# A two-layer hybrid decoder trunk on one core: order of the up-projection's matmuls, time of the parameter loads, queue of the output stores

## The chip, the core and the metric

One core of a Trainium2 chip runs the whole program. The metric is the time of one execution on the device in microseconds (us), as the median of several runs. A profile of one execution stands beside it; its span (from the first to the last instruction) is a little shorter than the execution's time.

## What is computed

The input x has 256 rows (positions) of 1024 numbers. Cut to what matters:

```
layer 0:  h = rmsnorm(x) ; u = h @ ab_w_in        # 1024 -> 2560 columns
          ya = conformer_conv(u_val, u_gate)      # GLU, causal conv of width 31, layernorm, silu
          yb = attention(q, k, v)                 # 8 heads of 64, causal, ALiBi
          x = x + concat(ya, yb) @ ab_w_out
          x = x + square(relu(rmsnorm(x) @ w_up[0])) @ w_down[0]      # 1024 -> 4096 -> 1024
layer 1:  h = rmsnorm(x) ; gate, xr = split(h @ c_w_in)
          xr = conv of width 4 ; y = rg_lru(xr) * gelu(gate)
          x = x + y @ c_w_out
          x = x + square(relu(rmsnorm(x) @ w_up[1])) @ w_down[1]
out = rmsnorm(x)
```

All in float32. With 256 rows there is one attention block, so no past blocks are selected.

## The kernel before, in words

**Planner.** The body of `hybrid_trunk` doesn't issue instructions. Each helper (`mms`, `tt`, `act`, `move`, `dma`, ...) adds an operation to a `Plan` with its engine, operands and an estimated cost. `Plan.schedule` (line 132) simulates the engines, lets each one pick the ready operation of highest rank, and `emit` issues everything in the order found. SP's DMAs alone keep the order in which they were added. So a moved line in the body moves work on every engine only as far as the planner's ranks let it. Nearly all instructions are issued at line 312, so rows of the profile are told apart by their tiles.

**Layout.** Activations lie transposed, as eight chunks (`xT[k]`, 128 channels x 256 positions). Weights come by SP's queue in pieces of 1 MB into the five `raw` tiles (or into pairs of `wh` and `wl`). Where a piece is split, ScalarE or VectorE rounds it into `wh` (fp32r) and VectorE puts the rest into `wl` (lines 588 to 592). The activations are split in the same way into a high and a low half, which lie side by side in one tile (`split_act`, line 701). A product is then three terms: high x wh, low x wh, high x wl.

**MLP (lines 982 to 1011).** For each of 32 groups f of 128 hidden channels, `project_wide` (line 695) makes the up-projection: for each of the eight chunks one matmul of 512 columns (`wh` against high and low side by side) and one of 256 columns (`wl` against high), both into one PSUM bank (bank_b). VectorE and ScalarE then make the activation. Four groups later the down-projection of the group (`down_mm`, line 1019) follows: twelve matmuls of 512 columns, three for each of four blocks, into four standing accumulators (bank_a). The last four groups' down-projection (`TAIL`) is done block by block behind the loop: 48 matmuls. In rows of the profile, `bank_b<-x,wh` with 512 columns and `bank_b<-x,wl` with 256 are the up-projection, `bank_a<-wh,f` and `bank_a<-wl,f` the down-projection; the layer-1 projections have `bank_b<-x,wh` with 256 columns.

**Start (lines 653 to 678, 738 to 750, 795 to 802).** SP loads x in four parts (arena), each followed by a part of the first gate and value weights. GpSimd's queue issues nine small loads, which wait for nothing but two memsets: the convolution's weights into `wrow`, eight vectors of parameters into rows of `prow`. TensorE transposes x chunk by chunk (`x_chunk`, line 739; bank_a<-ident,arena) and multiplies each chunk into the first gate and value units (bank_b<-xg,raw). Then it transposes `wrow` and `prow` into one bank, from which VectorE copies them into columns (`wcol`, `pcol`).

**End (lines 1212 to 1229).** The last down-projection goes block by block; each half row block of the output is scaled and stored by two DMAs on SP's queue:

```
        act(xg[:, :512], xg[:, :512], AF.Copy, scale=fc[:, 6:7])
        stt(xg[:, 512:], b, fc[:, 6:7], gfin[:, 512:], OP.mult, OP.mult)
        for h in (slice(0, 512), slice(512, D)):
            dma(o_dst[:, t, h], xg[:, h], P * 2048)
```

Of the kernel before, what the change touches and what calls it, by code (L numbers as in the profile page):

```python
# [11 lines left out]
P = 128  # L12
S = 256
D = 1024
KD = D // P
NF = 4096 // P
CONVW = 31
# [4 lines left out]
ARENA = 10496  # L22


WARM, XP, SIDE = 10, 4, (0, 0, 0, 0)


SETS = {AF.Exp: "exp", AF.Tanh: "exp", AF.Sqrt: "sqrt", AF.Silu: "silu",
# [288 lines left out]
def fsize(ap):  # L317
    n = 1
    for d in ap.shape[1:]:
        n *= d  # L320
    return n


def is_psum(ap):
    return str(ap.space).endswith("PSUM")
# [3 lines left out]
def hybrid_trunk(ctx, tc, x, mix_norm, mlp_norm, w_up, w_down, ab_w_in, ab_conv_w, ab_ln_g, ab_ln_b,  # L329
# [3 lines left out]
    plan = Plan(nc)  # L333
# [4 lines left out]
    def tl(name, shape=(P, S), dt=F32):  # L338
        return sb.tile(list(shape), dt, name=name)
# [23 lines left out]
    def vcost(n, fast=False, ap=False):  # L363
        return 0.066 + n * (0.00052 if fast else 0.001042) + ((0.105 if fast else 0.062) if ap else 0.0)

    def tt(out, a, b, op, engs="V"):
        n = fsize(out)
        cost = {}
        if "V" in engs:
            cost["V"] = vcost(n)  # L370
        if "G" in engs:
            cost["G"] = 0.135 + n * 0.0021
        return plan.add(engs, [("tensor_tensor", (out, a, b), {"op": op})], [out], [a, b], cost)

    def stt(out, a, s, b, op0, op1):
        ins = [a, b] + ([s] if isap(s) else [])
        return plan.add("V", [("scalar_tensor_tensor", (out, a, s, b), {"op0": op0, "op1": op1})], [out], ins,
                        {"V": vcost(fsize(out), ap=isap(s))})
# [9 lines left out]
    def copy(out, a):  # L388
        return plan.add("V", [("tensor_copy", (out, a), {})], [out], [a], {"V": vcost(fsize(out), not is_psum(a))})

    def move(out, a, scale=None):

        n, ap, far = fsize(out), scale is not None, not is_psum(a)

        def go(e, sub):
            if e is nc.scalar:
                return e.activation(sub(out), sub(a), AF.Copy, **({"scale": scale} if ap else {}))  # L397
            return e.tensor_scalar(sub(out), sub(a), scale, None, op0=OP.mult) if ap else e.tensor_copy(sub(out), sub(a))  # L398

        return plan.add("VA", [(go, (), {})], [out], [a] + ([scale] if ap else []),  # L400
                        {"V": vcost(n, far, ap), "A": (0.092 if far else 0.05) + n * 0.000833 + 0.093 * ap}, AF.Copy)
# [12 lines left out]
    def memset(out, v, engs="G"):  # L414
        return plan.add(engs, [("memset", (out, v), {})], [out], [], {engs: 0.1 + fsize(out) * 0.0005})

    def mms(items, after=()):

        calls, outs, ins, c = [], [], [], 0.0
        for o, l, r, st, sp in items:  # L420
            calls.append(("matmul", (o,), {"lhsT": l, "rhs": r, "start": st, "stop": sp, "skip_group_check": True}))
            outs.append(o)
            ins += [l, r]
            c += max(fsize(r) / 2400.0, 0.0533) * (1 if l.dtype == F32R else 4) + (0.0135 if l.dtype == F32R else 0.005)
        return plan.add("T", calls, outs[:1], ins, {"T": c}, after=after)

    def transposes(items):
        calls = [("transpose", (o, i, d), {}) for o, i, d in items]
        return plan.add("T", calls, [items[0][0]], [i for _, i, _ in items] + [items[0][2]],
                        {"T": 0.109 * len(items)})  # L430
# [3 lines left out]
        return plan.add("T", [("matmul", (out,), {"lhsT": in_, "rhs": ident, "start": first, "stop": False, "is_transpose": True,  # L434
                                                  "skip_group_check": True})], [out], [in_, ident], {"T": 0.109})

    def small_dma(out, in_):

        return plan.add("G", [("dma_start", (out, in_), {})], [out], [in_], {"G": 0.55}, lag=4.0)

    def dma(out, in_, size):
        return plan.add("S", [("dma_start", (out, in_), {})], [out], [in_], {"S": 0.0}, size=size)


    ident = tl("ident", (P, P))
    ones = tl("ones", (P, P))
    pcol = tl("pcol", (P, P))
# [26 lines left out]
    def ar(*shape):  # L474
        n = 1
        for d in shape:
            n *= d
        assert top[0] + n <= ARENA, top[0] + n
        a = arena[:, top[0]:top[0] + n]
        top[0] += n  # L480
        if len(shape) == 2:
            a = a.rearrange("p (a b) -> p a b", a=shape[0])
        return a
# [20 lines left out]
    def bank(tag):  # L504
        t = banks[tag][bank_at[tag] % len(banks[tag])]
        bank_at[tag] += 1
        return t
# [135 lines left out]
    xrow = [ar(2, D // XP) for _ in range(XP)]  # L643
    xall = arena[:, base0:base0 + 2 * D].rearrange("p (h t d) -> p h t d", h=XP, t=2)
    mrow, prow, wrow, scr, diag = ar(P), ar(P), ar(P), ar(XP, D // XP), ar(2, P)
    xsrc = x[0].rearrange("(t p) d -> p t d", p=P)
    R = lambda ap: ap.rearrange("a (b p) -> (a b) p", p=P)
# [13 lines left out]
    b = bank("b")  # L661
# [5 lines left out]
        mms([(warm[:, :P], ones, ones, True, True)])  # L667
    memset(prow, 0.0)
    memset(wrow, 0.0)
    small_dma(wrow[:CONVW * 4], R(ab_conv_w[0]))  # L670
    col0 = {"mix": 0}
    r0 = 16
    for name, ap, n in (("mlp", R(mlp_norm), 16), ("lng", R(ab_ln_g), 4), ("lnb", R(ab_ln_b), 4),
                        ("cw", R(c_conv_w[0]), 32), ("cb", R(c_conv_b), 8), ("br", c_b_r[0], 8),
                        ("bi", c_b_i[0], 8), ("lam", R(c_lambda), 8)):
        small_dma(prow[r0:r0 + n], ap)
        col0[name] = r0
        r0 += n

    def par(name, c):  # L680
        i = col0[name] + c
        return pcol[:, i:i + 1]
# [12 lines left out]
    def project_wide(b, u, xs):  # L695

        w = weights(u)
        for k in range(KD):
            mms([(b, w[0][:, k, :], xs[k][2], k == 0, False), (b[:, :S], w[1][:, k, :], xs[k][0], False, k == KD - 1)])

    def split_act(src, scale, tag, bufs, engs="V"):
        t = rot(tag, bufs, (P, 2 * S), F32R)
# [9 lines left out]
    def scaled(src, scale):  # L712
        t = rot("xg", KD)
        move(t, src, scale)
        return t
# [22 lines left out]
    xs = {}  # L738
    def x_chunk(k):
        b = bank("a")  # L740
        transposes([(b[:, t * P:(t + 1) * P], xrow[k * XP // KD][:, t, k % (KD // XP) * P:(k % (KD // XP) + 1) * P], ident) for t in range(2)])
        xs[k] = scaled(b[:, :S], par("mix", k))
        move(xT[k], b[:, :S])

    for k in range(KD):
        x_chunk(k)
    vgb = {0: (bank("b"), bank("b"))}
    for k in range(KD):
        for b, u in zip(vgb[0], (u_gate[0], u_val[0])):
# [16 lines left out]
    def gate_tail(c):  # L766
        gt = gts[c % 2]
        tt(gt, vgb[c][0][:, :S], rstd, OP.mult)
        act(gt, gt, AF.Tanh, scale=0.5)
# [4 lines left out]
    def val_tail(c):  # L774

        stt(gts[c % 2], gts[c % 2], 1.0, rstd, OP.add, OP.mult)
        tt(z[:, c, CONVW - 1:], vgb[c][1][:, :S], gts[c % 2], OP.mult)

        aside = SIDE[c]
        for j in range(CONVW):  # L780
            src = z[:, c, j:j + S]
            w = wcol[:, j * 4 + c:j * 4 + c + 1]
            if j < aside:
                t = yside[c % 2] if j == 0 else prod[j % 3]
                act(t, src, AF.Copy, scale=w)
                if j:
                    tt(yside[c % 2], yside[c % 2], t, OP.add, "G")
            elif j == aside:
                ts(y[c], src, w, None, OP.mult)
            else:  # L790
                stt(y[c], src, w, y[c], OP.mult, OP.add)
        if aside:
            tt(y[c], y[c], yside[c % 2], OP.add)

    b = bank("a")
    for t in range(2):
        mms([(b[:, t * P:(t + 1) * P], ones, diag[:, t], t == 0, True)])
    transposes([(b[:, 256:384], wrow, ident)])
    transposes([(b[:, 384:512], prow, ident)])
    copy(rstd, b[:, :S])  # L800
    ts(wcol, b[:, 256:384], 0.5, None, OP.mult)
    copy(pcol[:, 16:], b[:, 400:512])
    gate_tail(0)
    val_tail(0)

# [91 lines left out]
    for i in range(4):  # L899
        weights(u_v[i])  # L900
        n, j = units[u_v[i]]
        w = homes[n][j].rearrange("p (a b) -> p a b", a=2)
        for a in range(2):
            k = 2 * i + a
# [73 lines left out]
    xs = {}  # L978
# [58 lines left out]
    xs = {}  # L1037
# [11 lines left out]
    for n, block in enumerate(blocks):  # L1049
        t, c0, c1, b = block  # L1050
# [137 lines left out]
    xs = {}  # L1188
# [22 lines left out]
    o_dst = out[0].rearrange("(t p) d -> p t d", p=P)  # L1211
    for n, block in enumerate(blocks):
        t, c0, c1, b = block
        xg, fc = xg2[t], fcol[:, t]
        for i in range(len(us)):
            down_mm(block, ws[i], hs[i], False, i == len(us) - 1)

        part = fc[:, n % 2:n % 2 + 1]
        act(fsq, b, AF.Square, accum=part)
        if c0 == 0:  # L1220
            tt(xg[:, :512], b, gfin[:, :512], OP.mult)
            ts(fc[:, 4:5], part, 1.0 / D, EPS, OP.mult, OP.add)
            continue
        act(fc[:, 5:6], part, AF.Sqrt, scale=1.0 / D, bias=fc[:, 4:5])
        recip(fc[:, 6:7], fc[:, 5:6])
        act(xg[:, :512], xg[:, :512], AF.Copy, scale=fc[:, 6:7])
        stt(xg[:, 512:], b, fc[:, 6:7], gfin[:, 512:], OP.mult, OP.mult)
        for h in (slice(0, 512), slice(512, D)):
            dma(o_dst[:, t, h], xg[:, h], P * 2048)
    hybrid_trunk.plan = plan.emit(renew)  # L1230


# [29 lines left out]
```

## Time and profile before

| | |
|---|---|
| median of 3 runs | 573.44 us (573.37 to 573.73) |
| the profiled execution | 573.54 us |
| its span | 571.8 us |
| TensorE busy (matmuls; weight loads) | 563.5 us (99%); 480.8 us (84%) |
| VectorE, ScalarE, GpSimd busy | 434.4, 301.8, 7.5 us |
| DMA | 98.70 MB, mean 173 GB/s |

Busy times of TensorE are of modelled ends, so the pace of matmuls is read from the distance of their starts. A chain of waits is followed back from the last instruction to what released each one.

### The profile page before, as it was taken

To read this page: it belongs to the slowest core of one execution; us is meant where nothing else is said; L and a number is where in the kernel's file an instruction comes from. 1 tells how busy PE (TensorE), PEld (TensorE's weight loads), DVE (VectorE), ACT (ScalarE), POOL (GpSimd) and SP (SyncE) were. 2 spreads that over 40 slices of the span, in tenths; PEclk is the share of its full clock that TensorE was granted. 3 is DMA by queue.
4 is the path that set the end of the run, shared out by engine and by line. 5 is a ranking of instruction groups with operands and counts; after the bars stand their busy time and mean duration, and the time that the engine had idled before them with its cause. 6 is when DMAs were issued, how large, how long until landed. Compare 5 with 4: busy or idle time off the path is not lost.

```text
span 571.8 us, 8523 instructions
## 1 busy us (share of the span) xinstructions
PE 563.5 (99%) x2985; PEld 480.8 (84%) x2985; DVE 434.4 (76%) x987; ACT 301.8 (53%) x618; POOL 7.5 (1%) x31
## 2 busy tenths in 40 slices
PE   8999999999999999999999999999999999999995
PEld 7888759988888888888889999888888888888884
DVE  2899998889767677777739997979776777777732
ACT  5104134657555555555538799637455555555523
POOL 5000000000000000000000000000000000000000
PEclk9999999999999999999999999999999999999999
DMA  8991593415665466555009746955545664662001
GB/s 237 306 379 42 160 317 113 147 40 183 192 219 178 156 202 211 169 184 184 0 2 287 229 144 209 367 201 173 196 149 186 212 192 147 202 229 86 1 0 74
DMA packets 71738, 98.70 MB, mean 173 GB/s; under 512 B 3368, under 2 KB 59776, under 8 KB 71696
## 3 DMA queue, kind: packets, MB, share of 16 engines
q1 hardware_dynamic: 71408, 98.06, 53.2%
q8 instruction: 23, 0.38, 0.3%
q0 software_dynamic: 288, 0.11, 0.1%
q14 instruction: 19, 0.16, 0.1%
HBM read 97.11 MB, written 1.05 MB: 172 GB/s over the span
## 4 chain that ended last, share of the span: by engine, by line
PE 97%; DMA 1%; SPq 1%; DVE 0%; issue 0%; ACT 0%; DVEq 0%; ACTq 0%
PE bank_b L312 53%; PE bank_a L312 44%; DMA arena<-in_x_dram 1%; SPq L312 1%; DVE arena L312 0%; DVE x L398 0%; DVE x L312 0%; ACT tiny L312 0%; ACT arena L312 0%; DVE tiny L312 0%; DVEq L398 0%; ACTq L312 0%
## 5 line engine op out<-in xcount | busy, mean ns | idle before, releaser
L312 DVE TENSOR_TENSOR wl<-raw,wh 128x512 fp32r<-128x512 f32 x296 | 201.3, 689 | 78.3 <-ACT wh L397 65.6
L397 ACT ACTIVATE wh<-raw 128x512 fp32r<-128x512 f32 x259 | 160.9, 630 | 159.4 <-PE bank_b L312 95.2
L312 PE MATMUL bank_b<-x,wh 128*128 128x512 f32 (+1 forms) x768 | 230.5, 361 | 0.0
L312 PE MATMUL bank_b<-x,wl 128*128 128x256 f32 x640 | 179.6, 281 | 0.0
L312 PE MATMUL bank_a<-wh,f 128*128 128x512 f32 x512 | 160.2, 394 | 0.0
L312 PEld LDWEIGHTS bank_b<-x,wh 128*128 128x128 f32 x768 | 136.4, 189 | 23.4 <-DVE arena L312 0.2
L312 PEld LDWEIGHTS bank_b<-x,wl 128*128 128x128 f32 x640 | 121.1, 189 | 2.2
L312 PEld LDWEIGHTS bank_a<-wh,f 128*128 128x128 f32 x512 | 92.2, 188 | 19.4
L312 PE MATMUL bank_a<-wl,f 128*128 128x512 f32 x256 | 100.6, 393 | 0.0
L312 PEld LDWEIGHTS bank_a<-wl,f 128*128 128x128 f32 x256 | 48.0, 188 | 11.9
L312 DVE SCALAR_TENSOR_TENSOR arena<-arena,wcol 128x256 f32<-128x256 f32 x120 | 50.5, 478 | 0.2
L312 PE MATMUL bank_b<-xg,raw 128*128 128x256 f32 x160 | 35.8, 380 | 0.0
L312 PEld LDWEIGHTS bank_b<-xg,raw 128*128 128x128 f32 x160 | 29.9, 190 | 3.9
L312 ACT ACTIVATE relu<-relu 128x256 f32<-128x256 f32 x64 | 26.1, 410 | 12.4 <-DVE relu L312 12.2
L312 DVE TENSOR_TENSOR relu<-bank_b,relu 128x256 f32<-128x256 f32 x64 | 26.8, 418 | 5.0 <-ACT relu L312 5.0
L312 DVE TENSOR_TENSOR f<-relu,f 128x256 fp32r<-128x256 f32 x64 | 26.8, 422 | 2.2 <-ACT f L397 2.2
L312 DVE SCALAR_TENSOR_TENSOR relu<-relu,rstd 128x256 f32<-128x256 f32 x64 | 26.8, 425 | 1.8
L312 ACT ACTIVATE arena<-arena 128x256 f32<-128x256 f32 (+2 forms) x39 | 19.3, 521 | 16.8 <-DVE arena L312 15.6
L312 ACT ACTIVATE relu<-bank_b 128x256 f32<-128x256 f32 x64 | 23.6, 368 | 5.7 <-PE bank_b L312 5.7
L312 PE MATMUL bank_a<-arena,wl 128*128 128x256 f32 x96 | 26.3, 379 | 0.0
L312 PE MATMUL bank_a<-arena,wh 128*128 128x256 f32 x96 | 26.3, 378 | 0.0
L312 ACT ACT_TABLE_LOAD x17 | 21.8, 1283 | 1.9 <-PE bank_b L312 0.9
(127 smaller groups left out, 434.7 us busy)
## 6 DMA issues: line engine op xcount, KB each, us to landing
raw<-in_w_up_dram SPq DMA_DIRECT2D x64, 512.0 KB, 5.5
raw<-in_w_down_dram SPq DMA_DIRECT2D x64, 512.0 KB, 4.3
raw<-in_c_w_in_dram SPq DMA_DIRECT2D x16, 512.0 KB, 7.7
raw<-in_ab_w_in_dram SPq DMA_DIRECT2D x8, 512.0 KB, 7.7
wh<-in_ab_w_in_dram SPq DMA_DIRECT2D x5, 512.0 KB, 8.5
wl<-in_ab_w_in_dram SPq DMA_DIRECT2D x5, 512.0 KB, 8.6
raw<-in_ab_w_out_dram SPq DMA_DIRECT2D x4, 512.0 KB, 10.5
wh<-in_c_w_out_dram SPq DMA_DIRECT2D x4, 512.0 KB, 3.4
```

Of the source, the lines that this page charges most:

```text
L312: r.append(getattr(self.engines[o.eng], method)(*map(sub, a), **{n: sub(v) for n, v in k.items()}))
L397: return e.activation(sub(out), sub(a), AF.Copy, **({"scale": scale} if ap else {}))
```

## The change

In `project_wide` the wide and narrow matmuls of a unit are added in groups: wide ones in pairs, narrow ones in fours, all wide ones first. The nine small loads are added behind the chunks of x and wait for the transposes of chunk 5 (`LATE`); the transpose of `prow` gets a bank of its own and is added later. Of each row block's two stores, the first is issued by ScalarE's queue.

```
--- before.py
+++ after.py
@@ -22,7 +22,7 @@
 ARENA = 10496
 
 
-WARM, XP, SIDE = 10, 4, (0, 0, 0, 0)
+WARM, XP, SIDE, LATE = 10, 4, (0, 0, 0, 0), 5
 
 
 SETS = {AF.Exp: "exp", AF.Tanh: "exp", AF.Sqrt: "sqrt", AF.Silu: "silu",
@@ -434,9 +434,9 @@
         return plan.add("T", [("matmul", (out,), {"lhsT": in_, "rhs": ident, "start": first, "stop": False, "is_transpose": True,
                                                   "skip_group_check": True})], [out], [in_, ident], {"T": 0.109})
 
-    def small_dma(out, in_):
-
-        return plan.add("G", [("dma_start", (out, in_), {})], [out], [in_], {"G": 0.55}, lag=4.0)
+    def small_dma(out, in_, after=()):
+
+        return plan.add("G", [("dma_start", (out, in_), {})], [out], [in_], {"G": 0.55}, after=after, lag=4.0)
 
     def dma(out, in_, size):
         return plan.add("S", [("dma_start", (out, in_), {})], [out], [in_], {"S": 0.0}, size=size)
@@ -667,15 +667,7 @@
         mms([(warm[:, :P], ones, ones, True, True)])
     memset(prow, 0.0)
     memset(wrow, 0.0)
-    small_dma(wrow[:CONVW * 4], R(ab_conv_w[0]))
     col0 = {"mix": 0}
-    r0 = 16
-    for name, ap, n in (("mlp", R(mlp_norm), 16), ("lng", R(ab_ln_g), 4), ("lnb", R(ab_ln_b), 4),
-                        ("cw", R(c_conv_w[0]), 32), ("cb", R(c_conv_b), 8), ("br", c_b_r[0], 8),
-                        ("bi", c_b_i[0], 8), ("lam", R(c_lambda), 8)):
-        small_dma(prow[r0:r0 + n], ap)
-        col0[name] = r0
-        r0 += n
 
     def par(name, c):
         i = col0[name] + c
@@ -695,8 +687,10 @@
     def project_wide(b, u, xs):
 
         w = weights(u)
-        for k in range(KD):
-            mms([(b, w[0][:, k, :], xs[k][2], k == 0, False), (b[:, :S], w[1][:, k, :], xs[k][0], False, k == KD - 1)])
+        for k in range(0, KD, 2):
+            mms([(b, w[0][:, j, :], xs[j][2], j == 0, False) for j in (k, k + 1)])
+        for k in range(0, KD, 4):
+            mms([(b[:, :S], w[1][:, j, :], xs[j][0], False, j == KD - 1) for j in range(k, k + 4)])
 
     def split_act(src, scale, tag, bufs, engs="V"):
         t = rot(tag, bufs, (P, 2 * S), F32R)
@@ -738,12 +732,24 @@
     xs = {}
     def x_chunk(k):
         b = bank("a")
-        transposes([(b[:, t * P:(t + 1) * P], xrow[k * XP // KD][:, t, k % (KD // XP) * P:(k % (KD // XP) + 1) * P], ident) for t in range(2)])
+        turned = transposes([(b[:, t * P:(t + 1) * P], xrow[k * XP // KD][:, t, k % (KD // XP) * P:(k % (KD // XP) + 1) * P], ident) for t in range(2)])
         xs[k] = scaled(b[:, :S], par("mix", k))
         move(xT[k], b[:, :S])
+        return turned
 
     for k in range(KD):
-        x_chunk(k)
+        t = x_chunk(k)
+        if k == LATE:
+            turned = t
+
+    small_dma(wrow[:CONVW * 4], R(ab_conv_w[0]), [turned])
+    r0 = 16
+    for name, ap, n in (("mlp", R(mlp_norm), 16), ("lng", R(ab_ln_g), 4), ("lnb", R(ab_ln_b), 4),
+                        ("cw", R(c_conv_w[0]), 32), ("cb", R(c_conv_b), 8), ("br", c_b_r[0], 8),
+                        ("bi", c_b_i[0], 8), ("lam", R(c_lambda), 8)):
+        small_dma(prow[r0:r0 + n], ap, [turned])
+        col0[name] = r0
+        r0 += n
     vgb = {0: (bank("b"), bank("b"))}
     for k in range(KD):
         for b, u in zip(vgb[0], (u_gate[0], u_val[0])):
@@ -796,12 +802,13 @@
     for t in range(2):
         mms([(b[:, t * P:(t + 1) * P], ones, diag[:, t], t == 0, True)])
     transposes([(b[:, 256:384], wrow, ident)])
-    transposes([(b[:, 384:512], prow, ident)])
     copy(rstd, b[:, :S])
     ts(wcol, b[:, 256:384], 0.5, None, OP.mult)
-    copy(pcol[:, 16:], b[:, 400:512])
     gate_tail(0)
     val_tail(0)
+    b = bank("a")
+    transposes([(b[:, :P], prow, ident)])
+    copy(pcol[:, 16:], b[:, 16:P])
 
 
 
@@ -1225,8 +1232,8 @@
         recip(fc[:, 6:7], fc[:, 5:6])
         act(xg[:, :512], xg[:, :512], AF.Copy, scale=fc[:, 6:7])
         stt(xg[:, 512:], b, fc[:, 6:7], gfin[:, 512:], OP.mult, OP.mult)
-        for h in (slice(0, 512), slice(512, D)):
-            dma(o_dst[:, t, h], xg[:, h], P * 2048)
+        plan.add("A", [("dma_start", (o_dst[:, t, :512], xg[:, :512]), {})], [], [xg[:, :512]], {"A": 0.76})
+        dma(o_dst[:, t, 512:], xg[:, 512:], P * 2048)
     hybrid_trunk.plan = plan.emit(renew)
```

The order in which the engines get their instructions shows it at three places. On TensorE, in the MLP of layer 0, one up unit (bank_b, `x` are the split chunks) stood so before:

```order
L312 MATMUL bank_b_108<-x_130,wh_1_459 128x512
L312 MATMUL bank_b_108<-x_130,wl_1_633 128x256
L312 MATMUL bank_b_108<-x_131,wh_1_459 128x512
L312 MATMUL bank_b_108<-x_131,wl_1_633 128x256
L312 MATMUL bank_b_108<-x_132,wh_1_459 128x512
L312 MATMUL bank_b_108<-x_132,wl_1_633 128x256
L312 MATMUL bank_b_108<-x_133,wh_1_459 128x512
L312 MATMUL bank_b_108<-x_133,wl_1_633 128x256
```

and stands so now, the end of the eight wide ones, the eight narrow ones and the first of the down-projection:

```order
L312 MATMUL bank_b_108<-x_128,wh_1_459 128x512
L312 MATMUL bank_b_108<-x_129,wh_1_459 128x512
L312 MATMUL bank_b_108<-x_130,wl_1_633 128x256
L312 MATMUL bank_b_108<-x_131,wl_1_633 128x256
L312 MATMUL bank_b_108<-x_132,wl_1_633 128x256
L312 MATMUL bank_b_108<-x_133,wl_1_633 128x256
L312 MATMUL bank_b_108<-x_126,wl_1_633 128x256
L312 MATMUL bank_b_108<-x_127,wl_1_633 128x256
L312 MATMUL bank_b_108<-x_128,wl_1_633 128x256
L312 MATMUL bank_b_108<-x_129,wl_1_633 128x256
L312 MATMUL bank_a_104<-wh_1_977,f_137 128x512 x2
```

Every unit of both MLPs is regrouped in this way. On GpSimd's queue (POOL), at the start, the nine small loads pass behind two memsets:

```order
 L312 MEMSET arena 128x128 x2
+L312 MEMSET arena 128x4x30
+L312 MEMSET qs 64x1 x8
 L312 DMA arena<-in_ab_conv_w_dram 124x128
 L312 DMA arena<-in_mlp_norm_dram 16x128
```

They keep their order among themselves. On TensorE, at the start, behind the first gate and value units (bank_a_104 takes the row sums and the transposed `wrow`; bank_b_110 is the second gate unit):

```order
 L312 MATMUL bank_a_104<-arena,ones 128x128 x2
-L312 MATMUL bank_a_104<-ident,arena 128x128 x2
+L312 MATMUL bank_a_104<-ident,arena 128x128
 L312 MATMUL bank_b_110<-xg_118,raw_71 128x256
...
 L312 MATMUL bank_b_110<-xg_123,raw_71 128x256
 L312 MATMUL bank_b_110<-xg_124,raw_71 128x256
+L312 MATMUL bank_a_105<-ident,arena 128x128
 L312 MATMUL bank_b_110<-xg_125,raw_71 128x256
```

The transpose of `prow` leaves its place beside that of `wrow` and stands before the last matmul of the second gate unit.

## Rows read from the trace of the kernel before

**Rows 1.** Of the page, parts 1 and 4: busy times; shares of the chain by engine

```profile
PE 563.5 (99%) x2985; PEld 480.8 (84%) x2985; DVE 434.4 (76%) x987; ACT 301.8 (53%) x618; POOL 7.5 (1%) x31
...
PE 97%; DMA 1%; SPq 1%; DVE 0%; issue 0%; ACT 0%; DVEq 0%; ACTq 0%
```

**Rows 2.** The chain in order of time, MLP of layer 0: start, us, what

```profile
139.97 2.81 PE bank_b L312 x16
142.78 2.78 PE bank_a L312 x12
```

**Rows 3.** Busy time by stretch: us; PE, PEld, DVE, ACT, POOL busy; granted clock; DMA share, GB/s

```profile
123.00:137.00 14.00, 14.00 (x82) 12.29 (x81) 13.83 (x31) 11.12 (x24) 0.00 (x0) 1.00 0.48 154
...
139.81:285.24 145.43, 145.43 (x730) 122.20 (x729) 107.89 (x211) 79.18 (x159) 0.00 (x0) 1.00 0.53 170
403.85:549.28 145.43, 145.43 (x729) 122.19 (x728) 102.54 (x205) 76.83 (x154) 0.00 (x0) 1.00 0.47 153
```

**Rows 4.** Timeline, TensorE, 288 to 300 us: start, us, operation, shape, count

```profile
288.05 0.64 PE L312 MATMUL bank_a<-wh,f 128*128 128x512 f32 x2
288.52 0.40 PE L312 MATMUL bank_a<-wl,f 128*128 128x512 f32 x1
...
290.83 0.62 PE L312 MATMUL bank_a<-wh,f 128*128 128x512 f32 x2
...
298.76 0.39 PE L312 MATMUL bank_a<-wl,f 128*128 128x512 f32 x1
```

**Rows 5.** Timeline, TensorE, layer 1's projections: 256 columns alone

```profile
344.77 0.40 PE L312 MATMUL bank_b<-x,wh 128*128 128x256 f32 x2
...
346.21 0.40 PE L312 MATMUL bank_b<-x,wh 128*128 128x256 f32 x2
```

**Rows 6.** Timeline, TensorE, first up units of layer 0

```profile
125.19 0.39 PE L312 MATMUL bank_b<-x,wh 128*128 128x512 f32 x1
...
127.27 0.39 PE L312 MATMUL bank_b<-x,wh 128*128 128x512 f32 x1
```

**Rows 7.** The chain in order of time, the first down rows

```profile
137.22 2.75 PE bank_a L312 x12
```

**Rows 8.** Timeline, POOL, the first and the last of the nine small loads

```profile
1.75 0.67 POOL L312 DMA_DIRECT2D arena<-in_ab_conv_w_dram  x1 [0.17 <-POOL arena L312]
...
5.95 0.50 POOL L312 DMA_DIRECT2D arena<-in_c_lambda_dram  x1
```

**Rows 9.** The chain in order of time, start

```profile
5.77 4.93 DMA arena<-in_x_dram
```

**Rows 10.** DMA, first 30 us: packets, MB, engines' share; KB each, us to landing

```profile
DMA packets 12717, 8.26 MB, mean 275 GB/s; under 512 B 583, under 2 KB 12700, under 8 KB 12716
...
q0 software_dynamic: 288, 0.11, 1.8%
...
raw<-in_ab_w_in_dram SPq DMA_DIRECT2D x8, 512.0 KB, 7.7
...
arena<-in_c_lambda_dram POOLq DMA_DIRECT2D x1, 4.0 KB, 4.6
```

**Rows 11.** Timeline, TensorE, start

```profile
8.63 0.66 PE L312 MATMUL bank_a<-ident,arena 128*128 128x128 f32 x4
...
16.07 0.38 PE L312 MATMUL bank_a<-ident,arena 128*128 128x128 f32 x2
...
16.29 24.34 PE L312 MATMUL bank_b<-xg,raw 128*128 128x256 f32 x112
```

**Rows 12.** Timeline, all engines, end

```profile
567.26 0.72 ACT L312 ACTIVATE arena<-arena,tiny 128x512 f32<-128x512 f32 x1 [0.23 <-DVE tiny L312]
567.26 0.75 DVE L312 SCALAR_TENSOR_TENSOR arena<-bank_a,tiny,arena 128x512 f32<-128x512 f32 x1
568.01 0.81 SPq L312 DMA_DIRECT2D out_dram<-arena  x2
```

**Rows 13.** The output's tile: its four stores

```profile
DMA to landing us min/median/max: 2.0/2.2/2.3
```

## The prediction

> **What bounds the kernel now.** I read the page first: TensorE is busy for 99% of the span, and the chain of waits that ended last is 97% TensorE [rows 1]. So only three things can pay: a shorter pace of its matmuls, an earlier start, a shorter end. Next the chain in order of time, in the middle of an MLP: a piece of 16 matmuls into bank_b (one up-projection unit, line 699) takes 2.81 us, a piece of 12 into bank_a (one down-projection row block) 2.78 us, right behind it [rows 2]. The window from 139.81 us holds 26 such turns in 145.43 us, 5.593 us each, at a granted clock of 1.00, which is the 2.4 GHz level; in the other layer they take the same [rows 3]. One more turn follows in each layer, so 27 per layer, 54 in all. TensorE waits for nothing there, so the pace of each matmul is what counts, and I took it from the starts in the timeline.
>
> In the long run of 512-column matmuls at the end of an MLP, the first twelve take from 288.05 to 290.83, 231.7 ns each; the 35 from there to 298.76 take 226.6 ns each [rows 4]. So a wide matmul costs 227 ns, but after the switch from alternating work the first twelve together lose 2.78 - 12 x 0.2266 = 0.06 us. A 256-column matmul in a long run costs 120 ns: twelve from 344.77 to 346.21 [rows 5]. A pair should then cost 346.6 ns and eight pairs 2.773 us; the unit takes 2.81. The same alternation just after a wait does run at 346.7 (six pairs from 125.19 to 127.27 [rows 6]). Against these floors, 12 x 0.2266 + 8 x 0.3466 = 5.492 us, each turn loses 0.10 us: 0.06 in the down rows and 0.04 in the up unit. It is not the other engines' doing: the clean alternation at 125 us lies in a stretch where VectorE is busy for 13.83 of 14.00 us and ScalarE for 11.12 [rows 3].
>
> **The change, part by part.**
>
> *Order of the up units.* No matmul, weight load or column is added or removed. The order shows eight wide matmuls, then eight narrow, so the planner does what the diff asks. A turn becomes 12 wide (down), 8 wide and 8 narrow (up): one switch from narrow to wide instead of eight. What a switch costs behind eight narrow matmuls is shown nowhere. Bounds: 0.06 us, as now behind steady alternation [rows 4]; 0.03 us, as behind the clean alternation (twelve matmuls in 2.75 us, 2.72 without loss [rows 7]). I take 0.05: nearer the first, which is of the same unbroken stream, but the narrow run ahead of it runs clean [rows 5]. Then a turn costs 20 x 0.2266 + 8 x 0.120 + 0.05 = 5.542 us, 0.051 under 5.593, times 54: **-2.75 us**. With 0.03 it is 3.8, with no switch cost at all 0.10 x 54 = 5.4, and 0 if the loss is the turn's own. The five units ahead of the first down rows run clean in each layer [rows 6] and get a switch each, some 4 x 0.025 x 2 = **+0.2 us**.
>
> Here the Trainium skill speaks against the change: "TensorE: Matmul & The Clock Gate", section "Back-to-back issue gap", gives an isolated matmul N/2.4 plus 2.5 ns at the full clock, whatever stands before it; by that the order is worth nothing and this term is 0. The trace does not agree: 226.6 and 120 ns are each some 13 ns over N/2.4, and the same pair takes 346.7 or 351 ns by its surroundings.
>
> The narrow matmuls now have no wide one to cover their weight loads. That costs nothing more by [rows 5]: each of those has its own load too, and the pace is 120 ns.
>
> *Parameters behind six chunks.* Nine loads leave POOL's queue between 1.75 and 6.45 us [rows 8]. In that time x arrives, and on its fourth load (issued at 5.77, 4.93 us on the way) the start hangs [rows 9]. The nine loads are 0.11 MB and 1.8% of the 16 DMA engines' time in the first 30 us [rows 10], nearly all ahead of that landing: 0.11 MB at 275 GB/s is 0.40 us, 1.8% of 30 us is 0.54. If these packets only filled pauses, the gain is 0. I take **-0.45 us**, the middle of the two prices; behind x TensorE runs on without such a wait to the end, so all of it counts.
>
> What is late next: the loads now wait for the transposes of chunk 5, done at 8.63 + 0.66 = 9.3 us [rows 11]. Issues of 0.67 us for the first and some 0.50 for the others [rows 8] put the last at 9.3 + 0.67 + 7 x 0.50 = 13.5, and with the 4.6 us of the slowest now [rows 10] it lands at 18.1. Its reader, the transpose of prow, is moved behind seven of the eight gate matmuls (two records each, 112 records in 24.3 us, 0.217 each): 16.29 + 14 x 0.217 = 19.3 [rows 11]. Slack 1.2 us. The first load (wrow) is due at 16.07 and lands by 9.3 + 4.6 = 13.9. Behind the waiting POOL queue stand only the iota instructions, whose readers, the attention scores, come far later; the memsets of z and qs now go ahead. SP's queue keeps its order. Cost 0; bounds 0 and 2 us (a rival below).
>
> *Stores.* At the end both halves are ready together, ScalarE's at 567.26 + 0.72 and VectorE's at 567.26 + 0.75, but SP issues the two in 0.81 us, one behind the other [rows 12], and each lands 2.0 to 2.3 us after its issue [rows 13]. With one half on ScalarE's queue the second no longer waits 0.43 us. No row shows an issue on ScalarE; POOL's take up to 0.67 [rows 8] against half of 0.81 on SP, which would leave 0.1. I take **-0.4 us**, range 0.1 to 0.5. The first two stores lie beside matmuls, and ScalarE has nothing to do behind its own until the next block.
>
> **Sum:** -2.75 + 0.2 - 0.45 - 0.4 = -3.4. The profiled execution took 573.54 us (span 571.8, 1.7 outside), 0.1 over the median of the runs, 573.44. **Forecast 570.1 us.** About 0.2% (1.15 us) can be told from no change.
>
> **The rivals.**
>
> 1. *The loss is the turn's own:* one switch between a long narrow and a long wide run pays as much as eight do now. A turn stays at 5.59 and only start and end pay: 573.54 - 0.85 = 572.7. For it: the loss is the same in both layers to the last digit, as a fixed price would be. Against: the 35 clean matmuls [rows 4]. The additive rule of the skill cited above would end here too. 0.14.
>
> 2. *Wide matmuls behind a narrow run don't recover:* eight narrow ones build up more delay than one, and all 20 wide ones run as the dearest pair does now, 288.05 to 288.52, 235 ns each [rows 4]. Then a turn is 20 x 0.235 + 8 x 0.12 = 5.66, 0.067 over now, 54 times 3.6: 573.54 + 3.6 - 0.85 = **576.3**, slower. It decides, in the MLP stages, at a mean of (5.593 - 0.96) / 20 = 232 ns per wide matmul. Against it: the recovery within twelve. 0.07.
>
> 3. *No loss is left:* the single switch costs nothing among 20 wide matmuls: 573.54 - 5.4 - 0.85 = 567.3. Against it: every switch in an unbroken stream costs now. 0.10.
>
> 4. *Parameters too late:* the small loads now meet the weight loads, whose 512 KB take 7.7 us to land [rows 10]. At 13.5 + 7.7 = 21.2 TensorE has stood 2 us before prow's transpose, and VectorE's copy behind it: 570.1 + 2 = 572.1. Against: the nine met weight loads before too, and the slowest took 4.6 us. 0.07.
>
> That the order stays as it was is excluded by the order's rows.
>
> **How the numbers follow.** My forecast, with a switch anywhere from 0.03 to 0.08 us and the small terms at their bounds, holds 0.62 and 568.6 to 572.0. Rival 3 adds 0.10 below, rivals 1 and 4 put 0.21 at 572.1 to 572.7. The range 567.8 to 572.8 leaves out rival 2, the bottom of rival 3 and part of the late landings, some 0.2 together. Faster by over 0.2% (under 572.3): forecast, rival 3 and most of rival 4, 0.77; within 0.2%: 0.15; slower: 0.08.
>
> **What would show it.** The chain's pieces in an MLP: turns of 5.54 us (5.59: rival 1; above: rival 2; 5.49: rival 3). In the timeline, wide matmuls at 227 ns from about the twelfth of 20 on, narrow ones at 120. At the start the fourth x load landing near 10.3 instead of 10.7, and no wait before prow's transpose. At the end two issues side by side. I am wrong if the turn stays within 10 ns of 5.59, or if TensorE waits near 19 us.

## The result, and the profile after

The changed kernel takes 569.95 us (median of 4 runs, 569.68 to 570.22), the kernel before 573.59 (4 runs, 573.37 to 573.98) on the same chip: 0.9936 of the time, 95% interval 0.9919 to 0.9953. The forecast, 570.1 us, was right, and so was "faster by over 0.2%". That it fell so near is partly luck: one term was too small and two were wrong, as the runs below show.

The page of the kernel after, parts 1, 3 and 4 (against [rows 1]):

```profile
span 568.2 us, 8540 instructions
...
PE 558.8 (98%) x2985; PEld 481.6 (85%) x2985; DVE 427.1 (75%) x960; ACT 319.0 (56%) x643; POOL 7.4 (1%) x31
...
q10 hardware_dynamic: 288, 0.52, 0.2%
...
PE 93%; DMA 4%; SPq 1%; ACT 1%; issue 1%; DVE 0%; ACTq 0%; DVEq 0%
```

TensorE is still the bound, with the same 2985 matmuls. A new queue, q10, carries ScalarE's half of the output. The chain in order of time, MLP of layer 0 (start, us, what), and the busy time of 26 turns in either layer (us; PE, PEld, DVE, ACT, POOL busy; granted clock; DMA share, GB/s):

```profile
140.02 2.77 PE bank_b L312 x16
142.78 2.75 PE bank_a L312 x12
```

```profile
139.86:283.20 143.34, 143.34 (x729) 122.48 (x728) 101.69 (x186) 94.25 (x184) 0.00 (x0) 1.00 0.51 172
404.67:548.01 143.34, 143.34 (x730) 122.48 (x729) 100.49 (x203) 77.76 (x151) 0.00 (x0) 1.00 0.45 155
```

A turn is 143.34 / 26 = 5.513 us against 5.593 [rows 3]; both parts are shorter, the up unit (2.81 to 2.77) and the down rows, which the change does not touch (2.78 to 2.75) [rows 2]. The granted clock is 1.00 in both. In the first window the planner gave 25 pieces of VectorE's to ScalarE (x211 and x159 became x186 and x184); TensorE waits for neither there. Where the pace changes shows in TensorE's timeline, one turn:

```profile
200.50 1.98 PE L312 MATMUL bank_b<-x,wh 128*128 128x512 f32 x8
202.32 1.11 PE L312 MATMUL bank_b<-x,wl 128*128 128x256 f32 x8
203.27 0.63 PE L312 MATMUL bank_a<-wh,f 128*128 128x512 f32 x2
...
203.97 0.62 PE L312 MATMUL bank_a<-wh,f 128*128 128x512 f32 x2
...
204.66 0.62 PE L312 MATMUL bank_a<-wh,f 128*128 128x512 f32 x2
...
205.34 0.62 PE L312 MATMUL bank_a<-wh,f 128*128 128x512 f32 x2
...
206.02 0.84 PE L312 MATMUL bank_b<-x,wh 128*128 128x512 f32 x3
```

From start to start: eight wide in 1.82 us (227 ns each), eight narrow in 0.95 (119), then the down rows by threes in 0.70, 0.69, 0.68, 0.68. Behind the narrow ones the wide ones are slow within the first six and then run at 227. For twelve in a row that is 2.75 us against 2.72 at pace.

At the start and the end (all engines):

```profile
5.78 4.88 DMA arena<-in_x_dram
```

```profile
2.65 0.67 POOL L312 DMA_DIRECT2D arena<-in_ab_conv_w_dram  x1
...
7.08 0.50 POOL L312 DMA_DIRECT2D arena<-in_c_lambda_dram  x1 [0.23 <-DMA arena<-in_ab_conv_w_dram]
```

```profile
16.13 3.19 PE L312 MATMUL bank_b<-xg,raw 128*128 128x256 f32 x14
19.16 0.27 PE L312 MATMUL bank_a<-ident,arena 128*128 128x128 f32 x1
```

```profile
563.15 0.72 ACT L312 ACTIVATE arena<-arena,tiny 128x512 f32<-128x512 f32 x1 [0.23 <-DVE tiny L312]
563.15 0.75 DVE L312 SCALAR_TENSOR_TENSOR arena<-bank_a,tiny,arena 128x512 f32<-128x512 f32 x1
563.90 0.36 ACTq L312 DMA_DIRECT2D out_dram<-arena  x1
563.93 0.34 SPq L312 DMA_DIRECT2D out_dram<-arena  x1
```

x's fourth load lands at 5.78 + 4.88 = 10.66 us, before at 10.70 [rows 9], and not near 10.3. The small loads did not wait for chunk 5; they leave at 2.65 us, only behind the memsets that were moved ahead of them. At the end the two issues stand side by side, as meant, yet from the last scaling to the end of the span it is 568.2 - 563.15 = 5.05 us, where it was 571.8 - 567.26 = 4.5 [rows 12].

The account, by landmarks of both traces (change against before, us): second gate unit 16.13 (-0.16), first up unit 122.53 (-0.04), first down rows 137.11 (+0.05), end of the loop of layer 0 285.97 (-2.08), first down rows of layer 1 399.08 (-1.95), end of its loop 548.01 (-4.08), last scaling 563.15 (-4.11), end of span 568.2 (-3.6). Everything that was won is in the turns of the two MLPs, and half a microsecond was lost behind the last matmul.

### The profile page after: what moved, and what is told of

The parts are those of the page before. It is cut to its first block, busy times and chain, and to the rows that moved or that the text cites. A ratio compares the mean times of both kernels' runs of the same rounds, so it can differ in the third digit from the quotient of the medians.

```text
span 568.2 us, 8540 instructions
## 1 busy us (share of the span) xinstructions
PE 558.8 (98%) x2985; PEld 481.6 (85%) x2985; DVE 427.1 (75%) x960; ACT 319.0 (56%) x643; POOL 7.4 (1%) x31
## 4 chain that ended last, share of the span: by engine, by line
PE 93%; DMA 4%; SPq 1%; ACT 1%; issue 1%; DVE 0%; ACTq 0%; DVEq 0%
PE bank_b L312 50%; PE bank_a L312 43%; DMA raw<-in_c_w_in_dram 3%; SPq L312 1%; DMA arena<-in_x_dram 1%; ACT wh L397 0%; ACT L312 0%; DVE arena L312 0%; ACT arena L312 0%; DVE x L398 0%; ACT rstd L312 0%; DVE x L312 0%; ACT tiny L312 0%; DVE tiny L312 0%; DVE wl L312 0%
## 5 line engine op out<-in xcount | busy, mean ns | idle before, releaser
L312 DVE TENSOR_TENSOR wl<-raw,wh 128x512 fp32r<-128x512 f32 x296 | 195.2, 688 | 67.1 <-PE bank_b L312 42.5
L397 ACT ACTIVATE wh<-raw 128x512 fp32r<-128x512 f32 x286 | 174.6, 628 | 94.7 <-PE bank_b L312 43.0
L312 PE MATMUL bank_b<-x,wh 128*128 128x512 f32 (+1 forms) x768 | 175.0, 356 | 0.0
L312 PE MATMUL bank_b<-x,wl 128*128 128x256 f32 x640 | 107.5, 282 | 0.0
L312 PEld LDWEIGHTS bank_b<-x,wl 128*128 128x128 f32 x640 | 94.3, 190 | 5.0
L312 DVE TENSOR_TENSOR xT<-bank_a,xT 128x256 f32<-128x256 f32 x24 | 8.9, 419 | 15.8 <-PE bank_a L312 15.8
```

Of the source, the lines that this page charges most:

```text
L312: r.append(getattr(self.engines[o.eng], method)(*map(sub, a), **{n: sub(v) for n, v in k.items()}))
```

## The experiments

Each ran beside the kernel before on the same chip; ratios are to that, with 95% intervals.

### One part of the change at a time

**order_alone**: the kernel before with the new `project_wide`, nothing else.

```
-        for k in range(KD):
-            mms([(b, w[0][:, k, :], ...), (b[:, :S], w[1][:, k, :], ...)])
+        for k in range(0, KD, 2):
+            mms([(b, w[0][:, j, :], ...) for j in (k, k + 1)])
+        for k in range(0, KD, 4):
+            mms([(b[:, :S], w[1][:, j, :], ...) for j in range(k, k + 4)])
```

> The kernel before with the up units regrouped and nothing else. Theory (the order of the up units is the whole gain): a turn of an MLP takes 5.51 us as in the changed kernel, 54 turns x 0.08 give 4.3, the first units cost 0.2, so some 569.4 us, 0.3 to 0.6 below the changed kernel. Rival (the three parts share the gain): 571 or more, and the turn longer than 5.53 us.

569.3 us, 0.9918 [0.9905, 0.9931]; turn 5.513 as in the full change. The order alone gives all of the gain, as its theory had it.

**stores_alone**: the kernel before with ScalarE storing the first half.

```
-        for h in (slice(0, 512), slice(512, D)):
-            dma(o_dst[:, t, h], xg[:, h], P * 2048)
+        plan.add("A", [("dma_start", (o_dst[:, t, :512], xg[:, :512]), {})], ...)
+        dma(o_dst[:, t, 512:], xg[:, 512:], P * 2048)
```

> The kernel before with half of the output stored by ScalarE's queue and nothing else. Theory (two stores at once land later, and a second queue makes the end of the program longer): from the start of the last scaling to the end of the span 5.0 us instead of 4.5, so the time is 0.5 us longer, 574.0. Rival (the 0.5 us at the end of the changed kernel's profile is chance, the prediction's term holds): 0.4 us shorter, 573.1.

574.41 us, 1.0007 [0.9999, 1.0016]: the forecast gain of 0.4 us (a ratio of 0.9993) lies outside. The end, and the times from issue to landing of the output's four stores (min/median/max, us), which were 2.0/2.2/2.3 [rows 13]:

```profile
568.51 0.36 ACTq L312 DMA_DIRECT2D out_dram<-arena  x1
568.54 0.34 SPq L312 DMA_DIRECT2D out_dram<-arena  x1
```

```profile
DMA to landing us min/median/max: 2.6/2.7/2.8
```

The second issue no longer waits 0.43 us, and each of the last two transfers takes 0.5 to 0.6 us longer. From the last scaling to the end of the span it is 5.0 us, as the theory had it.

**params_alone**: the kernel before with the small loads added behind the chunks and the later transpose of `prow`.

```
+    small_dma(wrow[:CONVW * 4], R(ab_conv_w[0]), [turned])
...
+    b = bank("a")
+    transposes([(b[:, :P], prow, ident)])
```

> The kernel before with the nine small loads added behind six chunks of x and prow's transpose moved, nothing else. In the changed kernel's profile the loads start at 2.65 us, so they wait for two memsets and not for chunk 5. Theory (the wait exists in the planner alone): the loads start near 2.6 us again, the fourth x load lands near 10.7, the second gate unit starts 0.1 to 0.2 us earlier than before, time 573.3 to 573.5. Rival (the small loads are out of x's way): 573.0 or less.

573.71 us, 0.9998 [0.9989, 1.0006], and x's fourth load landed at 10.79 us: no gain. The loads leave from 2.65 us on here too, while x is still on its way, so this run does not show what they would cost x.

**real_wait**: the changed kernel, but `wrow` and `prow` are cleared by VectorE as zero times chunk 5, so that the loads into them must wait for it.

```
-    memset(prow, 0.0)
-    memset(wrow, 0.0)
...
+    for t in (wrow, prow):
+        ts(t, xT[LATE][:, :P], 0.0, None, OP.mult)
     small_dma(wrow[:CONVW * 4], R(ab_conv_w[0]), [turned])
```

> The changed kernel with the wait made real: VectorE clears wrow and prow with chunk 5's copy times zero, in place of the two memsets, so the loads can't start before chunk 5 is there. Theory (the small loads delay x, as the prediction had it): the fourth x load lands near 10.3, TensorE's second gate unit starts 0.3 to 0.5 us earlier than in the changed kernel, whose 569.95 us become 569.5. Rival A (the packets only fill pauses): x lands at 10.6 to 10.7 and the time stays. Rival B (parameters too late): TensorE stands before prow's transpose, 570.3 or more.

572.44 us, 0.9968 [0.9957, 0.9979]. Timelines of POOL and of TensorE:

```profile
11.41 0.67 POOL L312 DMA_DIRECT2D arena<-in_ab_conv_w_dram  x1 [9.00 <-DVE arena L312]
...
17.68 0.50 POOL L312 DMA_DIRECT2D arena<-in_c_lambda_dram  x1 [2.07 <-DMA arena<-in_ab_conv_w_dram]
```

```profile
10.91 0.63 PE L312 MATMUL bank_a<-ident,arena 128*128 128x128 f32 x4
...
17.44 0.33 PE L312 MATMUL bank_a<-ident,arena 128*128 128x128 f32 x1 [1.14 <-DMA arena<-in_ab_conv_w_dram]
...
23.20 0.33 PE L312 MATMUL bank_a<-ident,arena 128*128 128x128 f32 x1 [1.11 <-DMA arena<-in_c_lambda_dram]
```

Two things follow. With no small load under way before 11.41 us, x's fourth load landed at 10.78, not near 10.3, and its chunks were transposed from 10.91 (10.84 in the kernel before): the gain that was forecast did not come. That the loads take nothing at all from x is not shown by one landing. In the five kernels of this case whose loads leave from 1.75 us on, as before the change, the same landing lies anywhere from 10.28 to 11.15 us, a spread wider than the 0.45 us at stake.

And when the loads do wait, they come too late: TensorE stands 1.14 and 1.11 us, and the median is 2.5 us above that of the change as it is (runs from 570.66 to 573.22). That is the harm of rival 4, at nearly its price (2 us), but by another sum. The loads start at 11.41 us and not at 9.3, since VectorE's clearing stands before them; they land 5.3 to 6.0 us after their issue, not 4.6; and the ninth waits for the landing of the first. An estimate from these rows for a start at 9.3: the first lands at 15.3, the ninth is issued 0.3 us later and lands at about 21, some 1.7 us behind the 19.3 at which its reader is due. So the slack of 1.2 us in the prediction was not there.

### What costs at the end

Three kernels are the changed one with another split of the four stores. **no_store_change**: both halves by SP.

```
-        plan.add("A", [("dma_start", (o_dst[:, t, :512], xg[:, :512]), {})], ...)
-        dma(o_dst[:, t, 512:], xg[:, 512:], P * 2048)
+        for h in (slice(0, 512), slice(512, D)):
+            dma(o_dst[:, t, h], xg[:, h], P * 2048)
```

> The changed kernel with both halves of the output stored by SP again (order of the up units and late parameters kept). Theory: the new way of storing costs 0.5 us at the end (last scaling to end of span 5.0 us against 4.5 before), so this takes 569.95 - 0.5 = about 569.4 us, with 4.5 us from the start of the last scaling to the end of the span, and landings of 2.0 to 2.3 us. Rival: the longer end is chance of the one profiled execution; then it stays at about 570.0 us.

569.61 us (569.0 to 570.04), 0.9927 [0.9915, 0.9940]; 4.6 us from the last scaling to the end, as the theory had it. The time lies between the two forecasts and does not decide.

**act_first_block**: ScalarE stores one half of the first row block only.

```
+        if t == 0:
+            plan.add("A", [("dma_start", (o_dst[:, t, :512], xg[:, :512]), {})], ...)
+        else:
+            dma(o_dst[:, t, :512], xg[:, :512], P * 2048)
```

> The changed kernel with ScalarE storing only the first row block's first half; all of the last row block goes by SP. Theory A (what costs is that two queues store side by side at the very end): the end is as before the change, about 4.5 us from the last scaling to the end of the span, 569.4 us. Theory B (what costs is that the program has one more queue to close at its end, wherever it was used): 1.4 to 1.5 us from the last landing to the end of the span, as in the changed kernel, and 569.9 us or more.

569.62 us, 0.9932 [0.9919, 0.9944]; 4.8 us to the end, of which 1.38 lie behind the last landing. That is near B's sign; the time lies between the two and does not decide.

**act_both**: all four by ScalarE.

```
+        for h in (slice(0, 512), slice(512, D)):
+            plan.add("A", [("dma_start", (o_dst[:, t, h], xg[:, h]), {})], ...)
```

> The changed kernel with all four output stores issued by ScalarE, none by SP. Theory A (two queues side by side cost): one queue's landings take 2.0 to 2.3 us, the second issue follows the first by 0.4 us, end as before, 4.5 us, 569.4 us. Theory B (a store from ScalarE's queue is the slower thing, landing and closing): landings of 2.6 us or more and some 1.5 us after the last, the second 0.36 us later still, so 5.3 to 5.4 us, 570.3 us.

569.53 us, 0.9928 [0.9914, 0.9941]; 4.5 us to the end, and landings as from SP alone, which is theory A:

```profile
DMA to landing us min/median/max: 2.0/2.2/2.3
```

So ScalarE's queue is no slower than SP's, and two queues at once are what lengthens a landing. Why shows in the DMA share and rate (the last two columns) of the same stretches, first with both halves by SP (no_store_change, first issue at 563.95), then side by side (the changed kernel, 563.90):

```profile
563.90:564.90 1.00, 0.00 (x0) 0.00 (x0) 0.06 (x1) 0.02 (x1) 0.00 (x0) 0.93 0.12 45
564.90:565.40 0.50, 0.00 (x0) 0.00 (x0) 0.00 (x0) 0.00 (x0) 0.00 (x0) 0.50 1.03 385
565.40:566.00 0.60, 0.00 (x0) 0.00 (x0) 0.00 (x0) 0.00 (x0) 0.00 (x0) 0.50 1.01 379
566.00:566.80 0.80, 0.00 (x0) 0.00 (x0) 0.00 (x0) 0.00 (x0) 0.00 (x0) 0.50 0.25 85
```

```profile
563.90:564.90 1.00, 0.00 (x0) 0.00 (x0) 0.00 (x0) 0.00 (x0) 0.00 (x0) 1.00 0.12 45
564.90:565.40 0.50, 0.00 (x0) 0.00 (x0) 0.00 (x0) 0.00 (x0) 0.00 (x0) 1.00 1.03 393
565.40:566.00 0.60, 0.00 (x0) 0.00 (x0) 0.00 (x0) 0.00 (x0) 0.00 (x0) 1.00 1.01 382
566.00:566.80 0.80, 0.00 (x0) 0.00 (x0) 0.00 (x0) 0.00 (x0) 0.00 (x0) 1.00 0.20 67
```

Either way the first packets move 0.8 to 0.9 us after the first issue (from 564.78 and 564.76 on), and then all 16 DMA engines are full until 566. With both halves by SP the second issue was over by then, at 564.76, so there was no waiting that a second queue could take away. The Trainium skill, "DMA: Bandwidth & Descriptors", section "Issuing engines are not separate DMA queues", has DMAs from several engines interleave on the same 16 DMA engines, and only issue time saved by it. The trace agrees that the engines are shared, with 512 KB at 380 to 390 GB/s either way, and shows that here not even the issue time came back. From the first issue to the last landing it is 2.80 to 2.81 us in all six kernels that store the last row block side by side, and 2.69 to 2.71 in seven of the eight that store it from one queue (2.81 in no_store_change).

The other 0.44 us lies behind the last landing (566.70 + 1.50 = 568.2 us in the changed kernel; 570.70 + 1.06 before), most of it in one pause of 0.34 us between two of SP's last instructions. Of the kernels of this case the pause is in six that use ScalarE's queue (act_first_block among them, so it is no matter of two stores at the very end), but not in act_both, and not in narrow_first below, which stores as the changed kernel does. Its cause stays open.

### How the up unit may be ordered

Three kernels are the changed one with another order inside the unit. **narrow_first**: eight narrow, then eight wide.

```
+        mms([(b[:, :S], w[1][:, j, :], ...) for j in range(KD)])
+        mms([(b, w[0][:, j, :], ...) for j in range(KD)])
```

> The changed kernel with the eight 256-column matmuls of an up unit ahead of its eight 512-column ones, so that a turn is 8 narrow, 8 wide (up), 12 wide (down): one switch from narrow to wide as before, but inside the unit. Theory 1 (the loss counts the switches): a turn stays at 5.51 us, 570.0 us. Theory 2 (the loss sits at the boundary from narrow to wide of another unit, where the accumulating bank changes as well): the turn changes by up to 0.05 us, 54 x 0.05 = 2.7 us either way.

**two_switches**: 4 wide, 4 narrow, twice; **four_switches**: 2 and 2, four times (the same with steps of 2).

```
+        for k in range(0, KD, 4):
+            mms([(b, w[0][:, j, :], ...) for j in range(k, k + 4)] +
+                [(b[:, :S], w[1][:, j, :], ...) for j in range(k, k + 4)])
```

> The changed kernel with each up unit as 4 wide, 4 narrow, 4 wide, 4 narrow: two switches from narrow to wide in a turn. Theory 1 (every switch loses the same): the turn lies on the line from one switch (5.513 us) to eight (5.593), 5.513 + 0.080/7 = 5.524 us, and the kernel 54 x 0.011 = 0.6 us over the changed one. Theory 2 (only narrow matmuls standing alone between wide ones lose): 5.513 us, no difference.

> The changed kernel with each up unit as 2 wide, 2 narrow, four times over: four switches in a turn. Theory 1 (every switch loses the same): 5.513 + 3 x 0.080/7 = 5.547 us for a turn, the kernel 1.9 us over the changed one. Theory 2 (only narrow matmuls standing alone between wide ones lose): 5.513 us, no difference.

They took 570.8 us (0.9951 [0.9939, 0.9964]), 571.75 (0.9967 [0.9954, 0.9979]) and 569.69 (0.9929 [0.9915, 0.9944]). 26 turns of each, from the windows of narrow_first, two_switches and four_switches in this order:

```profile
141.11:284.46 143.35, 143.35 (x730) 122.48 (x728) 110.30 (x235) 67.24 (x131) 0.00 (x0) 1.00 0.50 173
```

```profile
139.69:283.90 144.21, 144.21 (x729) 122.24 (x728) 109.92 (x211) 77.29 (x159) 0.00 (x0) 1.00 0.53 171
```

```profile
140.01:283.18 143.17, 143.17 (x729) 121.78 (x728) 107.62 (x211) 79.26 (x159) 0.00 (x0) 1.00 0.53 173
```

Over the floor of 5.492 us, a turn loses:

| narrow matmuls of a unit stand | switches | turn, us | lost |
|---|---|---|---|
| singly (before) | 8 | 5.593 | 0.101 |
| in pairs | 4 | 5.507 | 0.015 |
| in fours | 2 | 5.547 | 0.055 |
| all eight, behind the wide ones | 1 | 5.513 | 0.021 |
| all eight, ahead of the wide ones | 1 | 5.513 | 0.021 |

Both theories fall. The loss does not count the switches: four cost less than one, two cost more. Nor is it only the lone narrow matmul that loses: those in fours lose too. Where the one switch stands does not matter (the last two lines). Nor is the cause the 25 pieces that the changed kernel moved from VectorE to ScalarE: four_switches has VectorE's x211 and ScalarE's x159 as before the change [rows 3], and the shortest turn.

The distances of the starts, as means over 25 turns, show where the loss sits. Behind eight narrow matmuls the wide ones take 233, 236, 228, 232 and 231 ns and then 227, some 0.03 us in all; the first two narrow ones behind wide ones at pace take 113 and 119 against 120, which gives 0.01 back. Behind the first four of two_switches it begins in the same way (233, 236, 228, 233), so four leave no more than eight. But only four wide ones follow there, and the next narrow run begins before the pace is back. Its up unit, by fours:

```profile
200.70 1.07 PE L312 MATMUL bank_b<-x,wh 128*128 128x512 f32 x4
201.61 0.64 PE L312 MATMUL bank_b<-x,wl 128*128 128x256 f32 x4
202.08 1.09 PE L312 MATMUL bank_b<-x,wh 128*128 128x512 f32 x4
203.01 0.63 PE L312 MATMUL bank_b<-x,wl 128*128 128x256 f32 x4
```

The first four wide ones take 0.91 us, the second four 0.93. Behind the second four narrow ones the down rows then need nine matmuls to come back to 227, by threes:

```profile
203.48 0.63 PE L312 MATMUL bank_a<-wh,f 128*128 128x512 f32 x2
...
204.19 0.62 PE L312 MATMUL bank_a<-wh,f 128*128 128x512 f32 x2
...
204.88 0.62 PE L312 MATMUL bank_a<-wh,f 128*128 128x512 f32 x2
```

0.71 and 0.69 us; in four_switches, behind a pair:

```profile
203.36 0.62 PE L312 MATMUL bank_a<-wh,f 128*128 128x512 f32 x2
...
204.05 0.62 PE L312 MATMUL bank_a<-wh,f 128*128 128x512 f32 x2
...
204.73 0.62 PE L312 MATMUL bank_a<-wh,f 128*128 128x512 f32 x2
```

0.69 and 0.68: two matmuls of 232 and 231, then 227. So what a turn loses depends on the lengths of the narrow and of the wide runs together, and no run here varies one of them alone. What in TensorE does this, no run here shows.

narrow_first keeps the turn and yet is 0.85 us slower. Its first up unit needs all eight chunks of the split x within 1 us, and the seventh is late:

```profile
124.33 0.79 PE L312 MATMUL bank_b<-x,wl 128*128 128x256 f32 x2 [0.51 <-ACT x L397]
```

Its first two units take 6.81 us against 5.77. With the wide ones first the changed kernel shows no wait there. The rest of the difference is small or goes the other way: from the last scaling to the end narrow_first takes 4.6 us against 5.05, without the pause on SP.

### The best version

**four_alone** is the kernel before with only the units' order, in pairs (stores and parameters as before); **order_again** repeats order_alone beside it.

```
+        for k in range(0, KD, 2):
+            mms([(b, w[0][:, j, :], ...) for j in range(k, k + 2)] +
+                [(b[:, :S], w[1][:, j, :], ...) for j in range(k, k + 2)])
```

> The kernel before with only the up units changed, to 2 wide, 2 narrow, four times over (the order with the shortest turn so far, 5.507 us); stores by SP and early parameters as before. If the terms add: 5.593 - 5.507 = 0.087 us for a turn, times 54 = 4.7 us, less 0.2 for the first units: 573.6 - 4.5 = about 569.1 us, 0.3 under the eight-wide-eight-narrow order alone. Rival: the 0.36 us between the two orders is lost elsewhere (first units, waits for pieces), and both take the same.

> The eight-wide-eight-narrow order alone, once more, beside the other on the same chip: 569.3 us, 0.5 to 0.7 under the whole change, if the late parameters give nothing and the new way of storing costs 0.4 to 0.5; 570.0 if that difference was chance.

568.82 us (568.6 to 569.41), 0.9914 [0.9900, 0.9927], and 569.13 us (569.09 to 569.57), 0.9919 [0.9906, 0.9933]. 26 turns of four_alone, then of order_again:

```profile
139.60:282.80 143.20, 143.20 (x729) 121.77 (x728) 107.68 (x211) 79.28 (x159) 0.00 (x0) 1.00 0.54 173
```

```profile
139.58:282.92 143.34, 143.34 (x729) 122.48 (x728) 101.72 (x186) 94.23 (x184) 0.00 (x0) 1.00 0.50 173
```

From the first matmul of the first turn to that of the 27th it is 143.17 us in four_alone (139.63 to 282.81) and 143.34 in order_again, so 0.007 us a turn, the same as between four_switches and the changed kernel; the times agree with that but don't prove it alone. Both medians lie under that of the changed kernel, which is the order plus two parts that give nothing or cost; the intervals overlap with its 0.9919 to 0.9953.

## Why the prediction was right, and where its steps were not

- **What bounds the kernel, and the floor of a turn:** right. The 226.6 and 120 ns of long runs [rows 4, 5] held in every order, and no turn went below 5.492 us.
- **The order's term, -2.75 us:** right in kind and too small: it is (5.593 - 5.513) x 54 = -4.3. The step that failed is the cost of a switch behind eight narrow matmuls, taken as 0.05 (bounds 0.03 to 0.06) from what the down rows lost behind steady alternation; it is 0.021, under both bounds: 0.03 in the wide ones, as in the lower bound, less 0.01 that the first two narrow ones give back. The loss behind alternation is no price of one switch, as the table shows, so it could not be carried over. The outcome of this term lies nearer to rival 3 (no loss left, 5.49) than to the forecast (5.54).
- **First units, +0.2:** right. From the first up unit to the first down rows 14.58 us against 14.49 in layer 0, +0.09, and 16.24 against 16.17 in layer 1, +0.07.
- **Rival 1, and the rule of the Trainium skill beside it:** the isolated gap of "TensorE: Matmul & The Clock Gate", section "Back-to-back issue gap", depends on the column count alone and would give the same time in any order; the table has five orders and four turns, 5.507 to 5.593. That section of the Trainium skill gives the formula for an isolated matmul and sets a stream of weight loads and matmuls apart from it; what runs here is such a stream, 2985 of each [rows 1]. Rival 2 (wide matmuls that don't recover) is out too: they recover within six.
- **Parameters, -0.45:** wrong in three places. The loads were said to wait for chunk 5: the order's row showed them behind two memsets only, and a place in the planner's order is no wait on the chip where no data passes between the two. And the price was of time taken from x's landing: in real_wait the landing came no earlier with the loads out of the way, so nothing speaks for a gain, though the scatter of that landing is too wide to put it at exactly 0. The slack of 1.2 us failed as well, by the loads' landing (5.3 to 6.0 us, not 4.6) and the ninth's wait; it cost nothing only because the loads did not wait. Small movements of the start remain (the first up unit began between 122.14 and 123.00 us in the kernels without real_wait), but early and late parameters lie mixed in them.
- **Stores, -0.4:** wrong sign, about +0.5 in the profile of after, and 0.34 us between the medians of after and no_store_change, whose runs overlap. The step that failed is "each lands 2.0 to 2.3 us after its issue", carried over to two issues at once; it is 2.6 to 2.8. From the first issue to the last landing that gains nothing or costs 0.1; the rest lies behind the last landing, most of it the pause on SP.
- **The sum:** -4.3 + 0.2 + 0 + 0.5 = -3.6, forecast -3.4. A term too small by 1.5 was met by two that gave nothing or cost, 0.85 in all forecast as gain and 0.5 as loss found. That they nearly cancel is luck. A forecast that hits by such a sum has not been understood until its parts have run alone.

## What to carry to other kernels

Where the chain is all matmuls, compare the pace of mixed shapes with that of long runs of each; what lies between is to be had by order alone, and the grouping that gives most must be tried (here pairs and eights, not fours). Before giving a transfer a second queue, look when the second issue ends: if it is over before the first transfer's packets leave the DMA engines free, as here, the second queue has nothing to bring forward. And in this planner a moved instruction waits on the chip only if it shares data with what it is moved behind, or stands behind other work on its own engine's queue, as the loads did behind two memsets.

## What was not expected of the hardware

- The loss of mixing 512- and 256-column matmuls: 0.101, 0.015, 0.055 and 0.021 us a turn for narrow runs of 1, 2, 4 and 8, to the same 0.001 us in both layers of a kernel.
- Two 256 KB stores at once from two queues land 2.63 and 2.78 us after issue, from one queue 2.02 and 2.27 (SP, before) or 2.03 and 2.32 (ScalarE, act_both).
- The ninth small load of GpSimd's queue started only as the first landed (0.23 us of waiting in the changed kernel, 2.07 in real_wait). By the trace it waits for the semaphore on which the first counts its landing, and counts its own on the same one: the program takes eight in turn for these loads. So this is the program's doing, and no run shows a limit of the queue itself.
